# A hybrid decoder layer on one core: in the last block, the last head's scan begun behind its keys, and two heads' output gates projected last

## The chip, the cores and the metric

The kernel runs on one core of one Trainium2 chip. The metric is the device time of one execution in microseconds (us). The core has five engines that run side by side, each in the order of its own instruction queue: TensorE (PE in the profile; its weight loads are PEld) multiplies matrices into PSUM, VectorE (DVE) and ScalarE (ACT) do elementwise work, GpSimd (POOL) does elementwise work in SBUF, and SyncE (SP) issues most of the transfers. ACT issues some transfers as well. An engine waits for another through semaphores; an instruction that waits holds everything behind it in its queue.

## The reference, cut to what matters

One decoder layer over 2048 tokens and 16 meta tokens ahead of them, width 1024, all in float32. The normalized input is projected to everything that two branches and their merge gates need; the branches are a Mamba-2 scan (16 heads) and gated linear attention, GLA (4 heads). Here only GLA matters:

```python
u = rmsnorm(hres, norm_w)
z, xbc, dt_raw, q, k, v, g_gla, a_lr, merge_g = split_cols(u @ w_in, IN_WIDTHS)
log_a = log_sigmoid(a_lr @ gla_gate_w2 + gla_gate_b) / 16
# per head (128 keys, 256 values), in chunks, with state S carried along the sequence:
#   S_t = diag(exp(log_a_t)) S_{t-1} + k_t^T v_t ;  o_t = q_t S_t
y_gla = rmsnorm(o, gla_norm_w) * silu(g_gla)
```

Each head so needs its queries and keys (q, k), its values (v) and its output gate (g_gla, 256 channels). The scan needs q, k and the decays first, v later, and the output gate only in its very last operation. The branch results then go through a second set of products: `sum_b sigmoid(g_b) * (y_b @ w_branch_b)`, `@ w_out`, residual and a last rmsnorm.

## The kernel before

**Two phases.** The first phase computes, in four blocks of 512 tokens, all projections but the merge gates', and both scans; it leaves the branch results (`y_left`) in DRAM. The second phase multiplies large matrices in stages (gate, branch 0, branch 1 for each half of the sequence, then out), with operands that it loads and prepares ahead (`load_a`, `prep_a`, `load_b`, `prep_b`). Each float32 operand is held as a high and a low part, and each product is three matmuls (`accum`, L188 to L190, which all products share in the profile: projections write `pj`, the scans write `pc`, the second phase `psa`, `psb`, `psc`).

**Order in a block.** Eight units follow each other: four groups of the Mamba branch, then four GLA heads, here called heads 0 to 3. Each unit is a generator of projection pieces (`gla_proj`); at each of its `yield`s the loop calls `step()`, which advances every running scan by one step. A scan is put on the list by `begin`. So PE's queue reads: a projection piece, then one step of each scan that runs, then the next piece. PE's and SP's order is the order in which the code is written; the order of ACT, DVE and POOL is set by a scheduler when the program is built, which moves instructions ahead where their operands allow it.

**A GLA head's projection.** Six pieces: queries (24 matmuls of 512 columns), keys (24), values in two halves (48 of 256 columns each), and two gate pieces (24 each). The weights come through four `whl` buffers. A gate piece ends in a tanh on ACT (L661) and a product on DVE (L662) into a `gg` tile, of which there are four. Only then is the head's scan begun.

**A GLA head's scan** (`gla_scan`), step by step: decays applied to keys and queries; six levels (64, 32, 16, 8, 4, 2), each with a subtraction on DVE (L711), two exponentials on ACT (L714, L715), products on DVE (L716, L718), two small matmuls on PE (L726) and a masked copy on DVE (L733); beside these the transposes of the decayed keys (L744) into two `kdt` tiles; pair and diagonal sums (L790), the masked attention, its transposes (L805), two `atp` tiles; then for each of four chunks a *c row*: six accumulations `pc<-tok,kdt` and `pc<-tok,atp`, one product with the state (L816), the state's update on DVE (L817), a copy on ACT (L819) and a sum of squares on ACT (L821). At the end `rstd` on DVE and POOL (L231, L232), a scaling on ACT (L826), eight transposes on PE (L831), the product with the gate on DVE (L832), and the store `y<-gg`, issued by ACT (L835).

PSUM is shared: three banks `pj`, three `pt` (transposes, L790), two `pc`. One scan holds both `kdt` and both `atp`.

**Into the second phase.** Its tiles lie on the first phase's memory. SP issues, behind the last weight, eight `ar` loads, then the `br` loads, of which five fit. POOL makes sums of `ar` (L944 to L947), ACT and DVE split them into high and low parts (L953, L954), and likewise `br` (L929, L930). The first product waits for the first `b`.

When the loop over the blocks has ended, `while running or begun: step()` runs what is left of the scans.

Of the kernel before, what the change touches and what calls it, by code (L numbers as in the profile page):

```python
# [40 lines left out]
def trunk_kernel(ctx: ExitStack, tc: tile.TileContext, xm, xmt, w_feat, w_tok, w_zm, w_br, w_o,  # L41
# [587 lines left out]
            nc.scalar.dma_start(y_left[0][o.b][2 * g + j], yo)  # L629


    def gla_proj(o, h):
        m0 = o.m0
# [8 lines left out]
        yield  # L642
        vh = mk(wk, [P, NCH, 256], F32R, "tok4", bufs=NT4)
        vl = mk(wk, [P, NCH, 256], F32R, "tok4", bufs=NT4)
        vm = None
        pss, places = halves_of(pj, "pj")
        if m0:
            vm = mk(wk, [P, 256], F32, "c1", bufs=NC1)[:META]
            pv5 = bank(pt, "pt")
            places.append((2, pv5[:, :256]))  # L650
        yield from proj_tok(f"v{h}", w_tok[SG + h], o.u, o.starts + [0] * o.ci0, places)
        if m0:
            nc.scalar.activation(vm, pv5[:META, :256], AF.Copy)
        for r, ps in enumerate(pss):
            split(*[t[:, 2 * r:2 * r + 2].rearrange("p c f -> p (c f)") for t in (vh, vl)], ps)
        yield
        gs = []
        for j in range(2):
            ps, = proj_feat(f"g{t0 + 2 + j}", w_feat[t0 + 2 + j], o.segs_real, o.mov)
            gg = mk(wk, [P, BLK], F32, "gg", bufs=4)  # L660
            nc.scalar.activation(gg, ps, AF.Tanh, scale=0.5)  # L661
# [3 lines left out]
        begin(gla_scan(o, h, qs, kf, (vh, vl), vm, gs))  # L665

    def gla_scan(o, h, qs, kf, vt, vm, gs):
        m0, tt = o.m0, o.tt
        gf = o.g_all[:, h, :tt]
        gr = gf[:, m0:]  # L670
# [79 lines left out]
        yield  # L750
        if m0:
            ps = bank(pc, "pc")
            nc.tensor.matmul(ps[:, :256], btm[:META], vm, start=True, stop=True)
            nc.vector.tensor_copy(s_gla[:, h], ps[:, :256])
        level_out(32)
        level_in(8)
# [53 lines left out]
        ssq = mk(sm, [P, 4], F32, "ssq")  # L810
        for c in range(NCH):
            po = bank(pc, "pc")
            vc = [t[:, c] for t in vt]
            accum(po[:, 256:], [t[:, c] for t in kdt], vc, True, True)
            accum(po[:, :256], [t[:, c] for t in atp], vc, True, False)
            nc.tensor.matmul(po[:, :256], qg[:, c * P:(c + 1) * P], s_gla[:, h], start=False, stop=True)  # L816
            nc.vector.scalar_tensor_tensor(s_gla[:, h], s_gla[:, h], egl[:, c:c + 1], po[:, 256:],  # L817
                                           op0=ALU.mult, op1=ALU.add)
            nc.scalar.activation(ot[:, c], po[:, :256], AF.Copy)  # L819
            jk = mk(wk, [P, 256], BF16, "junk", bufs=1)  # L820
            nc.scalar.activation(jk, po[:, :256], AF.Square, accum_out=ssq[:, c:c + 1])  # L821
            if c % 2:
                yield
        r = rstd_of(ssq, 4, 1.0 / 256)
        for c in range(NCH):
            nc.scalar.activation(ot[:, c], ot[:, c], AF.Identity, scale=r[:, c:c + 1])  # L826
        yield
        for j in range(2):
            ps = bank(pt, "pt")
            for c in range(NCH):  # L830
# [365 lines left out]
```

## Time and profile before

| | us |
|---|---|
| median of three timed runs | 2343.2 (2340.65 to 2347.39) |
| the profiled execution | 2339.3 |
| its span, first to last instruction | 2337.5 |
| PE busy | 2247.0 |
| DVE busy | 1572.1 |
| ACT busy | 1187.5 |
| POOL busy | 686.3 |
| mean granted clock of TensorE | 0.985 |

The span is what lies between the first and the last instruction; 1.8 us of the execution lie around it. Busy time is added up per engine, and engines overlap. A row of the timeline reads: start, duration, engine, line, operation, output and inputs, shape, count, and in brackets how long the engine had been idle before and what released it. A row of a group reads: line, engine, operation, tiles, shapes, count, then busy us and mean ns of one, then the idle time ahead of them and what ended it.

### The profile page before, as it was taken

How to read it: one execution, taken by the hardware profiler on the slowest of the kernel's cores; microseconds unless marked ns; L12 is line 12 of the kernel's file. 1: busy time of each engine (PE TensorE's matmuls, PEld its weight loads, DVE VectorE, ACT ScalarE, POOL GpSimd, SP SyncE). 2: the span in 40 equal slices, each digit the busy share in tenths (PEclk: the TensorE clock that was granted, in tenths of full speed). 3: DMA queues.
4: the chain of work that ended last, by engine and by line, in shares of the span. 5: the costliest groups of instructions: out<-in, count | busy, mean ns of one | idle time of the engine just before them, and what ended most of it. 6: DMA issues, size and time to landing. Idle time of an engine off the chain costs nothing.

```text
span 2337.5 us, 36518 instructions
## 1 busy us (share of the span) xinstructions
PE 2247.0 (96%) x12651; PEld 1961.9 (84%) x12651; DVE 1572.1 (67%) x2884; ACT 1187.5 (51%) x2764; POOL 686.3 (29%) x677
## 2 busy tenths in 40 slices
PE   6899999999999999999999999889999999999998
PEld 6889989888888989888988898768888788788786
DVE  5676766676675666576568555664588854788886
ACT  5666654465544455543465443454555454544443
POOL 3344433122221122222122200207433355332441
PEclk9999999999999999999999999989999999999999
DMA  7665865767785666786666645457668776778763
GB/s 256 222 204 199 295 232 200 227 197 235 249 284 185 210 214 216 247 271 210 201 222 217 207 162 168 140 165 235 215 226 281 270 232 204 257 250 279 237 199 108
DMA packets 300937, 515.89 MB, mean 221 GB/s; under 512 B 27616, under 2 KB 143584, under 8 KB 300752
## 3 DMA queue, kind: packets, MB, share of 16 engines
q1 hardware_dynamic: 200080, 401.17, 53.0%
q10 hardware_dynamic: 100672, 112.39, 13.9%
q8 instruction: 99, 1.62, 0.3%
q14 instruction: 86, 0.70, 0.1%
HBM read 366.26 MB, written 147.19 MB: 220 GB/s over the span
## 4 chain that ended last, share of the span: by engine, by line
PE 35%; DMA 7%; DVE 6%; issue 2%; ACT 2%; SPq 0%; POOL 0%; ACTq 0%; DVEq 0%; POOLq 0%
PE psa L188 4%; PE psa L189 4%; PE psa L190 4%; PE pj L188 4%; PE pj L190 4%; PE pj L189 4%; DMA br<-br_t 2%; PE psb L188 2%; PE psb L189 2%; PE psb L190 2%; DVE b L930 1%; DVE a L954 1%; PE psc L189 1%; PE psc L188 1%; PE psc L190 1%
## 5 line engine op out<-in xcount | busy, mean ns | idle before, releaser
L188 PE MATMUL pj<-u,whl 128*128 128x512 f32 (+1 forms) x1184 | 450.7, 381 | 16.1 <-ACT acc L502 8.9
L190 PE MATMUL pj<-u,whl 128*128 128x512 f32 (+1 forms) x1184 | 433.5, 366 | 0.6 <-POOL whl L176 0.6
L189 PE MATMUL pj<-u,whl 128*128 128x512 f32 (+1 forms) x1184 | 433.6, 366 | 0.0
L188 PE MATMUL pj<-whl,u 128*128 128x256 f32 (+1 forms) x992 | 289.0, 291 | 2.7 <-ACT u L251 2.2
L189 PE MATMUL pj<-whl,u 128*128 128x256 f32 (+1 forms) x992 | 282.3, 285 | 0.7 <-POOL whl L176 0.7
L190 PE MATMUL pj<-whl,u 128*128 128x256 f32 (+1 forms) x992 | 282.4, 285 | 0.2 <-DVE u L256 0.2
L188 PEld LDWEIGHTS pj<-u,whl 128*128 128x128 f32 x1184 | 227.5, 192 | 55.5 <-ACT acc L502 10.0
L188 PE MATMUL psa<-b,a 128*128 128x512 f32 x640 | 252.5, 395 | 15.4 <-ACT sn L970 13.5
L190 PEld LDWEIGHTS pj<-u,whl 128*128 128x128 f32 x1184 | 227.2, 192 | 36.8 <-POOL whl L176 0.8
L189 PEld LDWEIGHTS pj<-u,whl 128*128 128x128 f32 x1184 | 227.7, 192 | 33.5
L189 PE MATMUL psa<-b,a 128*128 128x512 f32 x640 | 251.3, 393 | 0.0
L190 PE MATMUL psa<-b,a 128*128 128x512 f32 x640 | 250.9, 392 | 0.0
L954 DVE TENSOR_TENSOR a<-ar,a 128x512 fp32r<-128x512 f32 x160 | 154.5, 972 | 76.6 <-ACT a L953 76.1
L80 POOL TENSOR_TENSOR wr<-wr 128x256 f32<-128x256 f32 x80 | 69.0, 862 | 434.6 <-DMA wr<-u 178.1
L188 PEld LDWEIGHTS pj<-whl,u 128*128 128x128 f32 x992 | 189.8, 191 | 4.0 <-ACT u L251 2.3
L176 POOL TENSOR_TENSOR whl<-wr,whl 128x512 fp32r<-128x512 f32 (+1 forms) x100 | 134.7, 1354 | 195.4 <-ACT whl L175 151.7
L189 PEld LDWEIGHTS pj<-whl,u 128*128 128x128 f32 x992 | 189.9, 191 | 1.3 <-POOL whl L176 0.9
L190 PEld LDWEIGHTS pj<-whl,u 128*128 128x128 f32 x992 | 189.7, 191 | 0.8 <-DVE u L256 0.8
L944 POOL TENSOR_TENSOR as<-ar,ar 128x512 f32<-128x512 f32 x40 | 59.8, 1494 | 416.5 <-DMA ar<-in_w_feat 123.7
L930 DVE TENSOR_TENSOR b<-br,b 128x512 fp32r<-128x512 f32 x196 | 149.3, 785 | 46.1 <-ACT b L929 45.5
L506 DVE SCALAR_TENSOR_TENSOR acc<-cin,hcw,acc 128x512 f32<-128x512 f32 (+1 forms) x192 | 155.4, 809 | 32.6 <-ACT acc L502 31.4
L929 ACT ACTIVATE b<-br 128x512 fp32r<-128x512 f32 x196 | 118.8, 626 | 92.9 <-DMA br<-br_t 35.3
(278 smaller groups left out, 5074.7 us busy)
## 6 DMA issues: line engine op xcount, KB each, us to landing
whl<-k_s SPq DMA_DIRECT2D x96, 512.0 KB, 4.3
whl<-k_g SPq DMA_DIRECT2D x96, 512.0 KB, 4.1
whl<-k_v SPq DMA_DIRECT2D x48, 512.0 KB, 4.3
whl<-k_z SPq DMA_DIRECT2D x36, 512.0 KB, 3.8
wr<-in_w_feat SPq DMA_DIRECT2D x64, 256.0 KB, 4.3
k_s<-whl SPq DMA_DIRECT2D x32, 512.0 KB, 3.7
cb<-cumd ACTq DMA_DIRECT2D x64, 256.0 KB, 5.7
y<-gg ACTq DMA_DIRECT2D x64, 256.0 KB, 4.3
```

The lines of the kernel that those rows point to most:

```text
L80: nc.gpsimd.tensor_tensor(o, x, y, op=ALU.subtract)
L176: nc.gpsimd.tensor_tensor(hl[:, 1], raw, hl[:, 0].bitcast(F32), op=ALU.subtract)
L188: nc.tensor.matmul(ps, sh, mh, start=first, stop=False, **kw)
L189: nc.tensor.matmul(ps, sh, ml, start=False, stop=False, **kw)
L190: nc.tensor.matmul(ps, sl, mh, start=False, stop=last, **kw)
L506: nc.vector.scalar_tensor_tensor(acc, cin[:, k:k + tt], hcw[:, ti, k:k + 1], acc, op0=ALU.mult, op1=ALU.add)
L929: nc.scalar.activation(t[:, 0], raw, AF.Copy)
L930: nc.vector.tensor_tensor(t[:, 1], raw, t[:, 0].bitcast(F32), op=ALU.subtract)
L944: nc.gpsimd.tensor_tensor(s1, a21, a22, op=ALU.add)
L954: nc.vector.tensor_tensor(t[:, 1], src, t[:, 0].bitcast(F32), op=ALU.subtract)
```

## The change

Only the last block's last two heads are touched, and only the order of their work. The projection of a head is cut into three generators (`gla_keys`, `gla_values`, `gla_gates`). Heads 0 and 1, and all heads of the other blocks, run as before. In the last block, head 2's scan is begun behind its values, with its gates not yet projected; head 3's scan is begun behind its keys; then follow head 3's values, head 2's two gate pieces and head 3's two gate pieces. The scan takes values and gates from a dictionary (`got`) that is filled by then.

```diff
+    def gla_proj(o, h):
+        got = {"gs": []}
+        keys = yield from gla_keys(o, h)
+        last = o.b == nblk - 1
+        if last and h == GH - 1:
+            begin(gla_scan(o, h, *keys, got))
+            yield
+            got["v"] = yield from gla_values(o, h)
+            yield
+            yield from gla_gates(o, h - 1, held_gates.pop())
+            yield from gla_gates(o, h, got["gs"])
+        else:
+            yield
+            got["v"] = yield from gla_values(o, h)
+            if last and h == GH - 2:
+                begin(gla_scan(o, h, *keys, got))
+                held_gates.append(got["gs"])
+                yield
+            else:
+                yield
+                yield from gla_gates(o, h, got["gs"])
+                begin(gla_scan(o, h, *keys, got))
...
-    def gla_scan(o, h, qs, kf, vt, vm, gs):
+    def gla_scan(o, h, qs, kf, got):
...
-            vc = [t[:, c] for t in vt]
+            vc = [t[:, c] for t in got["v"][0]]
...
+        gs = got["gs"]
         for j in range(2):
             ps = bank(pt, "pt")
```

In the changed kernel the lines of the scan stand 28 lower (29 from L826 on): L726 is L754, L790 is L818, L816 is L844, L819 is L847, L831 is L860, L953 is L982, L929 is L958. The text uses the numbers from before.

PE, from the last projection matmul of the first phase to the first product of the second, before; of each accumulation of three only the first row stands here:

```order
L190 MATMUL pj_16914<-u_11312,whl_16929 128x512
L805 MATMUL pt_16946<-cst,sq_16907 128x128 x2
L188 MATMUL pc_16953<-tok_2776_16232,kdt_16649 128x256
...
L744 MATMUL pt_17023<-cst,act_16977 128x128 x4
L726 MATMUL pc_17040<-sq_16992 128x128 x2
...
L831 MATMUL pt_17083<-cst,ot_16951 128x128 x4
...
L790 MATMUL pt_17138<-sq_17126,ones_r 128x512
L805 MATMUL pt_17149<-cst,sq_17142 128x128 x2
L188 MATMUL pc_17156<-tok_2851_16673,kdt_17028 128x256
...
L831 MATMUL pt_17217<-cst,ot_17154 128x128 x4
L188 MATMUL psa_17498<-b_2975_17403,a_17415 128x512
```

The same place now:

```order
L190 MATMUL pj_17101<-u_11312,whl_17116 128x512
L188 MATMUL pc_17142<-tok_2846_16605,kdt_16726 128x256
...
L844 MATMUL pc_17154<-s_gla,act_16593 128x256
L860 MATMUL pt_17166<-cst,ot_16994 128x128 x4
L860 MATMUL pt_17172<-cst,ot_16994 128x128 x4
L188 MATMUL pc_17178<-tok_2846_16605,kdt_16726 128x256
...
L844 MATMUL pc_17190<-s_gla,act_16593 128x256
L860 MATMUL pt_17211<-cst,ot_17140 128x128 x4
L860 MATMUL pt_17217<-cst,ot_17140 128x128 x4
L188 MATMUL psa_17498<-b_2975_17403,a_17415 128x512
```

Before, head 2's c rows and all of head 3's scan stood behind the last projection; now head 3's four c rows do, with the transposes of heads 2 and 3.

PE among the projections now, between the second half of head 3's values (`pj<-whl,u`) and head 2's first gate piece (`pj<-u,whl`); `pc_16818` is a c row of head 1, `pc_16830`, `pt_16834` and `pt_16837` belong to head 2, `pc_16848` to head 3:

```order
L844 MATMUL pc_16818<-s_gla,act_16136 128x256
L754 MATMUL pc_16830<-sq_16692 128x128 x2
L818 MATMUL pt_16834<-c_2864_16713,ones_r 128x256
...
L818 MATMUL pt_16837<-sq_16717,ones_r 128x512
...
L754 MATMUL pc_16848<-sq_16731 128x128 x2
...
L188 MATMUL pj_16872<-u_11312,whl_16873 128x512
```

Three scans now have a step between two projection pieces, where two had before.

ACT, from the third c row of head 3 to the first `b` of the second phase, now:

```order
L847 ACTIVATE ot_17140<-pc_17178 128x256
L849 ACTIVATE junk_17188,ssq_17141<-pc_17178 128x256
L982 ACTIVATE a_17426<-ar_17380 128x512
L982 ACTIVATE a_17441<-ar_17367 128x512
L982 ACTIVATE a_17452<-ar_17382 128x512
L982 ACTIVATE a_17467<-as_17374 128x512
L847 ACTIVATE ot_17140<-pc_17190 128x256
L849 ACTIVATE junk_17200,ssq_17141<-pc_17190 128x256
L854 ACTIVATE ot_17140<-ot_17140,rstd_17204 128x256 x4
L982 ACTIVATE a_17525<-as_17389 128x512
L982 ACTIVATE a_17543<-ar_17369 128x512
...
L958 ACTIVATE b_2975_17403<-br_17395 128x512
```

Before, these six preparations (L953 there) stood between head 2's c rows and head 3's levels, and no row stood between head 3's L819, L821 and L826.

More of the change, by code (lines that the diff above doesn't have):

```diff
@@ L641, in gla_proj, with gla_values @@
             nc.scalar.activation(kf[:, a:a + n], ps[:, :n], AF.Copy)
-        yield
+        return qs, kf
+    def gla_values(o, h):
+        m0 = o.m0
         vh = mk(wk, [P, NCH, 256], F32R, "tok4", bufs=NT4)
@@ L752, in gla_scan @@
             ps = bank(pc, "pc")
-            nc.tensor.matmul(ps[:, :256], btm[:META], vm, start=True, stop=True)
+            nc.tensor.matmul(ps[:, :256], btm[:META], got["v"][1], start=True, stop=True)
             nc.vector.tensor_copy(s_gla[:, h], ps[:, :256])
```

10 lines of the change are left out of this document (5 added, 5 removed).

## The prediction

> **What bounds the kernel now.** I read the page first, for the shares and the slices of the span.
>
> ```profile
> span 2337.5 us, 36518 instructions
> PE 2247.0 (96%) x12651; PEld 1961.9 (84%) x12651; DVE 1572.1 (67%) x2884; ACT 1187.5 (51%) x2764; POOL 686.3 (29%) x677
> PEclk9999999999999999999999999989999999999999
> ```
>
> TensorE (PE) is busy nearly everywhere, so what it must do sets the time; VectorE (DVE) and the others can matter only where PE waits for them. One slice has a lower clock. It is the seam between the first phase (projections and scans) and the second (the products of the gate stage), so I asked for busy time by stretch around it. The columns are stretch, length, then busy us of PE, its weight loads, DVE, ACT and POOL (instructions in brackets), granted clock, DMA share and GB/s.
>
> ```profile
> 1300.00:1400.00 100.00, 100.00 (x605) 89.18 (x604) 58.66 (x135) 48.19 (x124) 11.65 (x18) 1.00 0.57 187
> 1443.50:1500.50 57.00, 57.00 (x340) 50.59 (x340) 33.40 (x73) 20.64 (x56) 5.59 (x4) 1.00 0.59 190
> 1500.50:1526.50 26.00, 15.60 (x70) 12.41 (x69) 25.92 (x52) 14.45 (x40) 9.60 (x7) 0.74 0.14 51
> 1526.50:1544.80 18.30, 10.77 (x50) 8.42 (x48) 7.17 (x16) 6.20 (x20) 1.01 (x1) 0.75 0.10 35
> 1544.80:1580.00 35.20, 33.06 (x134) 26.24 (x135) 25.70 (x41) 25.09 (x46) 3.03 (x3) 0.94 0.86 270
> ```
>
> While there are projections PE has no gap (57.00 of 57.00 us) and DVE idles 23.6 us. In the 44.3 us behind them (the tail) PE is busy 26.4 us at a granted clock of 0.74 to 0.75; DVE is full in the first part of it and nearly empty in the second. PE's timeline shows what stands at the edges.
>
> ```profile
> 1500.32 0.39 PE L190 MATMUL pj<-u,whl 128*128 128x512 f32 x1
> 1500.55 0.38 PE L805 MATMUL pt<-cst,sq 128*128 128x128 f32 x2
> 1530.02 0.56 PE L188 MATMUL pc<-tok,kdt 128*128 128x256 f32 x1
> 1536.80 0.68 PE L816 MATMUL pc<-s_gla,act 128*128 128x256 f32 x2
> 1540.66 2.16 PE L831 MATMUL pt<-cst,ot 128*128 128x128 f32 x8 [3.19 <-ACT ot L826]
> 1544.78 0.80 PE L188 MATMUL psa<-b,a 128*128 128x512 f32 x1 [1.96 <-ACT b L929]
> ```
>
> The last projection matmul is followed at 1500.55 by scan work alone: the second half of head 2's scan and all of head 3's. The second phase's first product starts at 1544.78. The tail is a chain through DVE, ACT, POOL and PE, with nothing for PE to do beside it.
>
> **The change, part by part.** No arithmetic is removed or added. The same eight half-weights of head 2's and head 3's gates are loaded and the same matmuls run; they stand elsewhere. Head 2's scan starts behind its values, head 3's behind its keys, so six projection pieces (head 3's values in two halves, four gate pieces) now run beside head 3's scan. In the changed PE order only four c rows of head 3 (the accumulations at L188 to L190 and L816), eight transposes of head 2 and eight of head 3 (L831) stand behind the last projection.
>
> *First term, what PE takes in earlier.* These leave the tail: head 2's L805 and c rows, head 3's L744, its six levels (24 instructions of L726 in the trace), its L790 and L805. Their cost at full clock beside projections comes from starts in the same trace.
>
> ```profile
> 1443.57 1.04 PE L831 MATMUL pt<-cst,ot 128*128 128x128 f32 x8
> 1444.44 1.06 PE L726 MATMUL pc<-sq 128*128 128x128 f32 x8
> 1445.26 0.48 PE L188 MATMUL pj<-u,whl 128*128 128x512 f32 x1
> 1450.81 0.60 PE L726 MATMUL pc<-sq 128*128 128x128 f32 x4
> 1451.96 0.40 PE L188 MATMUL pj<-u,whl 128*128 128x512 f32 x1
> 1457.44 0.38 PE L805 MATMUL pt<-cst,sq 128*128 128x128 f32 x2
> 1457.58 0.48 PE L188 MATMUL pj<-u,whl 128*128 128x512 f32 x1
> 1463.13 0.28 PE L188 MATMUL pc<-tok,kdt 128*128 128x256 f32 x1
> 1465.35 0.58 PE L188 MATMUL pj<-u,whl 128*128 128x512 f32 x1
> 1470.99 0.28 PE L188 MATMUL pc<-tok,kdt 128*128 128x256 f32 x1
> 1473.39 0.60 PE L744 MATMUL pt<-cst,act 128*128 128x128 f32 x4
> 1473.83 0.61 PE L726 MATMUL pc<-sq 128*128 128x128 f32 x4
> ```
>
> Eight L726 take 0.82 us (1444.44 to 1445.26), so 24 take 2.46. L790 is 1450.81 to 1451.96 less four L726: 0.74. L805 is 0.14, twice 0.28. The c rows of one head are 2.22 (1463.13 to 1465.35) and 2.40 (1470.99 to 1473.39), together 4.62. L744 is 0.44. Sum 8.54. Without a stall the last projection would end at 1500.55 + 8.54 = 1509.1.
>
> *Second term, stalls of PE among the projections.* The two scans now run two steps apart instead of six, and share what holds one of them: two `kdt`, two `atp`, two `pc` banks, three `pt` banks. PE obeys its order, so whatever waits for a bank holds the projection behind it. In the changed order a level's L726 stands right behind a pair of c rows at three places, and its bank comes free only when ACT has read the c row before it (L819, L821). The gap can be read at the end of the tail and in the groups of waits.
>
> ```profile
> 1538.03 0.38 ACT L819 ACTIVATE ot<-pc 128x256 f32<-128x256 f32 x1 [0.52 <-DVE s_gla L817]
> 1538.31 0.38 ACT L821 ACTIVATE junk<-pc 128x256 bf16<-128x256 f32 x1
> L726 PEld LDWEIGHTS pc<-sq 128*128 128x128 f32 x24 | 3.8, 237 | 1.9 <-ACT junk L821 1.1 <-DVE c L733 0.8
> ```
>
> L816 starts at 1536.80 and lasts 0.68, L821 ends at 1538.69: 1.2 us, three times, is 3.6 us, and I take 4. Below it lies 0: PE's own work behind a c row covers the lag. Above it lies 10.4, PE's idle time in 1500.50:1526.50 (26.00 less 15.60), where c rows of one head and levels of the next last ran against each other with no projection between. I stay near the lower bound since projections now stand between. DVE's load speaks for that too: 33.40 + 25.92 + 7.17 = 66.5 us of DVE have to fit into some 80, and part of these is inflated by POOL.
>
> ```profile
> L711 DVE TENSOR_TENSOR sq<-g_all 128x512 f32<-128x512 f32 x5 | 5.6, 1117 | 0.0
> L711 DVE TENSOR_TENSOR sq<-g_all 128x512 f32<-128x512 f32 x8 | 6.6, 823 | 0.0
> L718 DVE TENSOR_TENSOR sq<-sq,act 128x128 f32<-128x128 f32 x12 | 6.1, 553 | 0.0
> L718 DVE TENSOR_TENSOR sq<-sq,act 128x128 f32<-128x128 f32 x12 | 2.9, 288 | 0.0
> 1498.73 1.36 POOL L945 TENSOR_TENSOR as<-as,ar 128x512 f32<-128x512 f32 x1
> ```
>
> The first row of each pair is the tail, the second the stretch ahead of it. Beside POOL's sums for the gate stage (the last row is one of eight; POOL is busy 9.60 us in 1500.50:1526.50) L718 took 553 ns against 288. These sums wait for `ar` loads that SP issues behind the last weight, and in POOL's new order they stand behind head 2's `rstd`. So the levels, which are through by then, lose this neighbour, and DVE's L954 in the new tail gets it.
>
> *Third term, the new tail.* From the last projection's end: four c rows and eight L831 at full clock, 4.62 + 0.87 (head 0's eight, 1443.57 to 1444.44) = 5.5 us. Then what follows the last c row now: its L816 ends at 1537.48, the first product starts at 1544.78, 7.3 us. Here ACT's order adds preparations of the second phase: four L953 ahead of the last L819, two between the last L826 and the store, and two L954 on DVE between the last L832s.
>
> ```profile
> 1512.08 1.15 ACT L953 ACTIVATE a<-ar 128x512 fp32r<-128x512 f32 x2
> 1514.07 1.29 DVE L954 TENSOR_TENSOR a<-ar,a 128x512 fp32r<-128x512 f32 x2
> 1542.23 1.41 DVE L832 SCALAR_TENSOR_TENSOR gg<-pt,hgw,gg 128x512 f32<-128x512 f32 x2 [3.25 <-PE pt L831]
> ```
>
> Two L953 take 1.15, so one every 0.52 to 0.58: four take 2.2, of which some 0.8 pass while the last c row runs, leaving 1.3 to 1.4. Two L954 take 1.29 between the L832s, nearly all on the chain. With 2.6 the new tail is 5.5 + 7.3 + 2.6 = 15.4 us. In the old order those seven L953 and L954 ran in the gaps of the tail; that cover is gone. Bounds: 12.8 if they hide again, 19 if the c rows run at the low clock (1530.02 to 1537.48 is 7.46, 2.8 us above 4.62) and POOL slows two L954 as it slowed L718.
>
> [...]
>
> [...]
>
> *SP and stores.* The chain of waits and ACT's timeline show a head's store and who waited for it.
>
> ```profile
> 1488.10 6.31 DMA y<-gg
> 1494.50 0.60 ACT L661 ACTIVATE gg<-pj 128x512 f32<-128x512 f32 x1 [7.02 <-DMA y<-gg]
> ```
>
> Weight loads of the moved gates are issued in the new order with four `whl` buffers as before; each has at least one projection piece (5.5 us) of lead. Head 1's store of `gg` must land before head 3's first gate can be written (L661); it waited 7.02 us in the old order without holding PE, and about 9 us of PE work (c rows 2.22, L726 and L790 1.15, a gate piece 5.5) lie between now. The first `br` loads wait for the last projection in both orders and have the tail to land in. I cost these at nothing; without the cover, one store's landing (6.31 us) would show.
>
> **The sum.** Last projection ends at 1509.1 + 4 = 1513.1; first product at 1513.1 + 15.4 = 1528.5 instead of 1544.78: 16.3 us less. What follows is the same work in the same order. Against the profiled execution (2339.3 us, span 2337.5) that gives 2323.0; the three timed runs lie at 2343.2 in the median, so 2327. With the bounds (stalls 0 to 10.4, tail 12.8 to 19) the gain is between 22.9 and 6.3; without the corners, 22 to 8: the forecast's own range is 2321 to 2335.
>
> **Rivals.**
> - *Clean overlap.* No stall, and the L953 hide: 1509.1 + 12.8 = 1521.9, 22.9 less, 2320.3. For it: DVE idles 23.6 us beside projections. Against it: two banks for two scans. Chance 0.09.
> - *Shared buffers eat most of it.* PE loses 10.4 to 14 us to banks and to DVE's levels, 2333 to 2337. For it: DVE at 25.92 of 26.00 where two scans met. Against it: 57 us of projections between them. Chance 0.15, about half of it beyond what can be told from no change.
> - *It does nothing.* DVE runs ahead already (levels of head 3 are part of the eight L711 in 1443.50:1500.50, ahead of the last projection's end); if DVE's chain sets the tail, the moved PE order only shifts waits: 2340 to 2345. Against it: DVE's 23.6 idle us. Chance 0.07.
> - *Slower: PE stands behind every level.* If each of the twelve levels of heads 2 and 3 must be waited out in order (subtract, two exponentials, three products: about 2.8 us, an estimate from L711, L718 and their neighbours), 12 × 2.8 = 34 us stand among the projections; the first product starts at 1509.1 + 34 + 15.4 = 1558.5, 14 us later, 2357. It decides from 1.7 us per level, where the stalls reach 20 us. For it: a `pt` bank is held from head 3's L744 until head 2 gives up `kdt`. Against it: DVE is asked a step (5 us or more) ahead. Chance 0.05.
>
> **How the numbers follow.** The forecast has 0.64. A measurement of this kernel tells 0.3% (7 us) from no change. Faster: 0.62 of the forecast, 0.09, 0.08 of the second rival and a little of the third, 0.80. Same: the rest of these, 0.14. Slower 0.06. For 8 in 10 the range takes in the clean overlap with some spread of runs (2340.65 to 2347.39 before) and most of the second rival: 2317 to 2339.
>
> **What would show it.** Right: the granted clock near 1.00 until about 1510; a stretch from the last `pj` matmul to the first `psa` of 14 to 17 us instead of 44.3; PE's idle among the projections 2 to 6 us, named by L726 waiting for L821 or L733. Wrong: gaps over 1.7 us ahead of each L726; a tail above 25 us; L661 waiting for the store with a `pj` matmul behind it; or a second phase that takes longer from its first product to the end.

## The result, and the profile after

The changed kernel took 2331.5 us in the median of 22 runs (2319.7 to 2345.2), the kernel before 2341.9 us in 22 runs beside it: a ratio of 0.9952, 95% interval 0.9939 to 0.9964. By the ratio that is some 11 us less; the medians differ by 10.4. A second measurement (10 runs against 18) gave 0.9958 (0.9943 to 0.9974). The forecast was 2327, some 16 us less; its range, 2317 to 2339, holds the result. The profiled execution took 2335.1 us.

The page of the profile after, shares of the span and TensorE's granted clock by slices:

```profile
span 2333.2 us, 36527 instructions
PE 2243.2 (96%) x12651; PEld 1957.1 (84%) x12651; DVE 1562.5 (67%) x2884; ACT 1188.5 (51%) x2764; POOL 680.4 (29%) x677
PEclk9999999999999999999999999999999999999999
```

PE's busy time is the same within 4 us. No slice shows a lower clock any more, though 10 us at half clock are left in the tail (the last section shows them). Around the seam, by stretch (columns as before: length, busy us of PE, weight loads, DVE, ACT and POOL, clock, DMA share, GB/s):

```profile
1443.23:1512.91 69.68, 67.89 (x408) 58.87 (x407) 47.59 (x119) 30.08 (x85) 4.44 (x4) 1.00 0.48 155
1512.91:1530.88 17.97, 8.66 (x49) 6.54 (x47) 10.83 (x18) 9.42 (x26) 8.54 (x8) 0.84 0.30 107
```

The first row starts at head 0's transposes, which stood at 1443.57 before, and ends behind the last projection; the second is the new tail. PE has 1.8 us of gaps in the first row and 9.3 in the second; before, it had none in 57 us and 17.9 in a tail of 44.3. PE's timeline of the changed kernel has the edges (lines are those of the changed kernel: L754 is L726 of before, L844 is L816, L849 is L821, L854 is L826, L860 is L831, L982 is L953):

```profile
1386.79 1.04 PE L626 MATMUL pt<-cst,tok 128*128 128x128 f32 x8
...
1468.81 0.71 PE L754 MATMUL pc<-sq 128*128 128x128 f32 x4 [0.56 <-ACT junk L849]
...
1512.68 0.39 PE L190 MATMUL pj<-u,whl 128*128 128x512 f32 x1
1512.91 0.28 PE L188 MATMUL pc<-tok,kdt 128*128 128x256 f32 x1
...
1517.37 0.38 PE L188 MATMUL pc<-tok,kdt 128*128 128x256 f32 x1 [0.92 <-ACT junk L849]
1519.34 0.70 PE L844 MATMUL pc<-s_gla,act 128*128 128x256 f32 x2
1524.88 2.53 PE L860 MATMUL pt<-cst,ot 128*128 128x128 f32 x8 [4.84 <-ACT ot L854]
1530.88 0.79 PE L188 MATMUL psa<-b,a 128*128 128x512 f32 x1 [3.47 <-ACT b L958]
```

The last projection ends at 1512.9 (forecast 1513.1) and the first product starts at 1530.88 (forecast 1528.5, before 1544.78). The first row is the landmark for all that follows: the last Mamba group's eight transposes, which stand ahead of anything that the change moves (1387.13 in the profile of before). Times counted from it are compared between kernels; of what lies ahead of it single executions differ by up to 15 us.

| us from the landmark to | last projection matmul | first product | third product (first `psc`) | first product of the branch stage | from the first product to the end |
|---|---|---|---|---|---|
| before | 113.2 | 157.7 | 165.4 | 317.6 | 792.7 |
| before, second profile | 113.2 | 158.8 | 167.2 | 320.1 | 800.6 |
| the change | 125.9 | 144.1 | 151.9 | 307.6 | 802.3 |
| the change, second profile | 125.9 | 144.1 | 152.0 | 306.8 | 799.2 |

So the first product comes 13.6 us sooner (14.7 against the second profile), the branch stage 10 to 13 us sooner, and the time falls by 11.

The gate stage lies between those two places. It took 163.5 and 162.7 us with the change, and 160.0 and 161.3 before: 1.3 to 3.5 us of the gain are lost there again. PE's waits name ACT, which reads the product banks (`sn`, L970): 6.3 and 6.5 us in the two profiles of the change, 4.1 and 3.7 us before, from 140 to 320 us behind the landmark. No run tested what makes these waits longer.

### The profile page after: what moved, and what is told of

The parts are those of the page before. It is cut to its first block, busy times and chain, and to the rows that moved or that the text cites. A ratio compares the mean times of both kernels' runs of the same rounds, so it can differ in the third digit from the quotient of the medians.

```text
span 2333.2 us, 36527 instructions
## 1 busy us (share of the span) xinstructions
PE 2243.2 (96%) x12651; PEld 1957.1 (84%) x12651; DVE 1562.5 (67%) x2884; ACT 1188.5 (51%) x2764; POOL 680.4 (29%) x677
## 4 chain that ended last, share of the span: by engine, by line
PE 60%; DMA 13%; DVE 10%; issue 7%; ACT 6%; POOL 3%; SPq 1%; ACTq 0%; POOLq 0%; DVEq 0%
PE pj L188 10%; PE pj L190 10%; PE pj L189 10%; PE psa L188 4%; PE psa L189 4%; PE psa L190 4%; DMA br<-br_t 2%; PE psb L190 2%; PE psb L189 2%; PE psb L188 2%; PE pc L754 1%; PE pc L591 1%; DMA acc<-in_xmt 1%; DMA br<-gate_t 1%; DVE b L959 1%
## 5 line engine op out<-in xcount | busy, mean ns | idle before, releaser
L983 DVE TENSOR_TENSOR a<-ar,a 128x512 fp32r<-128x512 f32 x160 | 155.2, 977 | 81.4 <-ACT a L982 80.9
L958 ACT ACTIVATE b<-br 128x512 fp32r<-128x512 f32 x196 | 118.5, 625 | 98.3 <-DMA br<-br_t 36.1
```

The lines of the kernel that those rows point to most:

```text
L958: nc.scalar.activation(t[:, 0], raw, AF.Copy)
L983: nc.vector.tensor_tensor(t[:, 1], src, t[:, 0].bitcast(F32), op=ALU.subtract)
```

## The experiments

The time of a whole run scatters by 10 us and more, so the parts are read at the four places of the table; the ratio of the timed runs stands beside them where there is one. The expectations count the runs in the order in which they were made, which is not the order of this text; what is called the third run, the seventh and the ninth is named by its edit too.

**Two halves.** First, head 2 alone: its scan behind its values, its gates last; head 3's scan behind its own gates as before.

```diff
-        if last and h == GH - 1:
+        yield
+        got["v"] = yield from gla_values(o, h)
+        if last and h == GH - 2:
             begin(gla_scan(o, h, *keys, got))
+            held_gates.append(got["gs"])
             yield
...
         else:
             yield
...
+            yield from gla_gates(o, h, got["gs"])
+            begin(gla_scan(o, h, *keys, got))
+            if last and h == GH - 1:
+                yield from gla_gates(o, h - 1, held_gates.pop())
```

> Only head 2 is changed: its scan begins behind its values and its gates are projected behind head 3's gates; head 3's scan begins behind its own gates as before. Measured from the last Mamba group's eight transposes (L626) to the first product of the second phase (the seam): 157.65 us before, 144.09 with the whole change. Theory (what stays behind the last projection costs the length of its chain, what goes beside projections costs PE's matmul time and a small stall): head 2's c rows go among the projections (4.8 us and about 1 of stall), head 3's whole scan stays in the tail (28.4 us in the profile of before, from its L744 to the first product, and about 1 for its first level): seam 148.6, between 146 and 151, some 9 us of gain. Rival (DVE's load sets the tail, so only taking head 3's levels out shortens it): seam at or above 154.

Last projection 120.4, first product 154.7, branch stage 315.5, ratio 0.9973 (0.9955 to 0.9991). The first product gains 3.0 us, not 9: the rival's number. DVE's timeline of this run shows what stood there, its tail starting at 1501:

```profile
1502.32 1.22 DVE L738 TENSOR_TENSOR sq<-sq,act 128x256 f32<-128x256 f32 x1
1503.46 1.55 DVE L740 TENSOR_TENSOR sq<-sq,act 128x128 f32<-128x128 f32 x2
...
1511.06 0.41 DVE L738 TENSOR_TENSOR sq<-sq,act 128x256 f32<-128x256 f32 x1
...
1512.20 0.48 DVE L740 TENSOR_TENSOR sq<-sq,act 128x128 f32<-128x128 f32 x2
```

DVE was busy 18.67 of the 20 us from 1501 on, most of it with head 3's scan. GpSimd's sums for the second phase ran from 1498.1 to 1508.7, and the first two rows, beside them, took three times what the last two took without. My 28.4 us for head 3's scan was counted from PE's first operation of it; in the profile of before DVE had begun these levels ahead of that, beside head 2's c rows.

Second, head 3 alone. Its scan begins behind the first half of its values. Directly behind its keys was not tried: it would run one step behind head 2's scan, and its transposes would stand in PE's queue ahead of the c rows of head 2 that free the `kdt` tiles. Head 3's early start as in the change needs head 2's.

```diff
+        yield
         if last and h == GH - 1:
+            values = gla_values(o, h)
+            next(values)
             begin(gla_scan(o, h, *keys, got))
             yield
+            got["v"] = yield from values
+        else:
             got["v"] = yield from gla_values(o, h)
...
+        yield
+        yield from gla_gates(o, h, got["gs"])
+        if not (last and h == GH - 1):
+            begin(gla_scan(o, h, *keys, got))
```

> Only head 3 is changed: its scan begins behind the first half of its values (behind its keys it would run one step behind head 2's scan, whose buffers it shares), head 2 is as before. Theory (length of the chain): two of head 3's three steps of levels go among the projections, head 2's c rows and head 3's stay in the tail one after the other; last projection about 2 us later, tail about 29 us: seam 145 to 148, some 10 to 12 us of gain. So the two halves do not add up: 9 and 11 alone, 13.6 together. Rival (each half has its own share of the 13.6 us): with the first run at 9, this one gains 4 to 5 and the seam is 153.

Last projection 117.5, first product 153.1, branch stage 316.5, ratio 0.9994 (0.9971 to 1.0017). The first product gains 4.6 us, again not my 10 to 12; the number is the rival's, but its premise, a gain of 9 us from head 2 alone, had failed. The two halves give 3.0 and 4.6 and the whole 13.6, so neither theory holds: the whole is more than its halves, and 6 us come only when both are there. DVE's timeline of this run shows the same neighbour:

```profile
1503.87 1.76 DVE L734 TENSOR_TENSOR sq<-g_all 128x512 f32<-128x512 f32 x1
1505.56 2.62 DVE L741 TENSOR_TENSOR sq<-sq,act 128x128 f32<-128x128 f32 x2
```

With either half alone some levels stay in the tail, beside GpSimd's sums. With both they are through before the sums begin, as DVE's last masked copy of a level and GpSimd's first sum show in the changed kernel:

```profile
1498.77 0.45 DVE L761 COPY_PREDICATED c<-msk,pc 128x256 f32<-128x256 uint8 x1 [0.31 <-PE pc L754]
```

```profile
1510.38 1.29 POOL L973 TENSOR_TENSOR as<-ar,ar 128x512 f32<-128x512 f32 x1
```

Beside the sums DVE's operations were longer than the same ones without by some 3.4 us in the first run and 6 us in the second (estimates, added up from their rows). So the sums can be a good part of what each half lacks; that they are all of it is not shown.

**The neighbour by itself.** The kernel before, with nothing moved but GpSimd's two sets of sums, which wait for head 3's `rstd`:

```diff
         r = rstd_of(ssq, 4, 1.0 / 256)
+        if o.b == nblk - 1 and h == GH - 1:
+            nc.gpsimd.tensor_tensor(behind, r, mhalf[:, :4], op=ALU.pow)
...
+            if self.name == "gate0" and n < 2:
+                nc.gpsimd.tensor_tensor(s1[:, 0, :4], behind, mhalf[:, :4], op=ALU.pow)
             nc.gpsimd.tensor_tensor(s1, a21, a22, op=ALU.add)
```

> The kernel before, with GpSimd's sums for the second phase (L944 to L947, two sets) held back behind head 3's rstd by two tiny operations on GpSimd; nothing else is moved. In the profile of before these sums run from 1497 to 1509 beside DVE's levels, and DVE's L711, L716, L718 and L237 took 11.4 us there that take 4.0 elsewhere. Theory (these 7.4 us are a part of the tail, and the change gained some of its 13.6 us by moving the sums off the levels): the stretch from the last projection to the first product falls from 44.5 to 37 to 39 us, seam (last L626 to first product) 150 to 152, about a half of the change's gain without the change. Rival (DVE's levels are hidden behind head 2's c rows there): seam 155 to 158.

First product 149.0, tail 35.6 us instead of 44.2: 8.7 us sooner without moving anything on PE, more than the 6 to 8 us that the theory gave. Groups on DVE, of before where the sums run beside the levels (1497:1509.1):

```profile
L711 DVE TENSOR_TENSOR sq<-g_all 128x512 f32<-128x512 f32 x3 | 4.2, 1404 | 0.0
L718 DVE TENSOR_TENSOR sq<-sq,act 128x128 f32<-128x128 f32 x4 | 4.2, 1086 | 0.0
```

and of this run at the same work (1498:1509.5; its lines are one higher), then where the sums run now (1537:1549, the preparation of the gate stage's `b`):

```profile
L712 DVE TENSOR_TENSOR sq<-g_all 128x512 f32<-128x512 f32 x5 | 3.4, 686 | 0.0
L719 DVE TENSOR_TENSOR sq<-sq,act 128x128 f32<-128x128 f32 x8 | 2.0, 287 | 0.0
...
L933 DVE TENSOR_TENSOR b<-br,b 128x512 fp32r<-128x512 f32 x8 | 10.3, 1361 | 0.0
```

And yet no change of the time shows: ratio 1.0003 (0.9984 to 1.0023). The third product gained 6.3 us of the 8.7, and the branch stage, at 316.0, 1.6 us (4.1 against the second profile of before). The sums had found another victim: L933 took 1361 ns beside them, and 688 ns per operation as the same group in the profile of before. That stands ahead of the third product; what takes back the rest in the gate stage was not traced. So part of the 13.6 us of the change is this: it takes the levels away from under the sums, and the sums then fall into a stretch where DVE is not full (10.83 of 17.97 us). How the 13.6 us divide between the two causes these runs do not say; the changed kernel with the sums held back was not run.

**The new tail** (the third run). The preparations of the second phase, which stood between head 3's last operations, asked for behind them: ACT and DVE are held to the order in which the code is written, in the end of the scans and in the first preparations. A third edit, not shown, writes the first preparation of `a` ahead of the first of `b`. As built, all but one stand behind head 3's stores.

```diff
+    with tc.manual_schedule(engines={mybir.EngineType.PE, mybir.EngineType.SP, mybir.EngineType.Activation,
+                                     mybir.EngineType.DVE}):
         while running or begun:
             step()
...
-        run(-1)
+        with tc.manual_schedule(engines={mybir.EngineType.Activation, mybir.EngineType.DVE}):
+            run(-1)
```

> The changed kernel, but ACT and DVE take the end of the scans and the preparations behind it in the order of the code: all L953/L954 but the first stand behind head 3's stores instead of between its last operations. Theory (the four L953 ahead of the last c row's copy cost 2.1 us and the two L954 between the last two gate products 1.8 us on the chain): the stretch from the last projection to the first product falls from 18.0 to about 14.1 us, seam 140.2 (139.5 to 141.5), and the gate stage's first products run up to 2 us slower for operands prepared later. Rival (they only fill time in which the chain waits for something else): seam 143 to 144.

Last projection 125.9 as with the change, first product 141.3, third 149.0, branch stage 302.6, ratio 0.9928 (0.9900 to 0.9956, from four runs). The first product is inside the theory's range. The tail falls by 2.8 of the 3.9 us expected, and the gate stage is not slower for it. ACT's and DVE's timelines of the changed kernel show what was removed, and one cost that I had not seen:

```profile
1513.60 0.62 ACT L982 ACTIVATE a<-ar 128x512 fp32r<-128x512 f32 x1
1516.53 0.38 ACT L847 ACTIVATE ot<-pc 128x256 f32<-128x256 f32 x1 [2.31 <-PE pt L860]
...
1519.96 1.67 ACT L982 ACTIVATE a<-ar 128x512 fp32r<-128x512 f32 x3
1521.52 0.62 ACT L982 ACTIVATE a<-as 128x512 fp32r<-128x512 f32 x1
1522.04 0.38 ACT L847 ACTIVATE ot<-pc 128x256 f32<-128x256 f32 x1
```

```profile
1520.08 0.48 DVE L845 SCALAR_TENSOR_TENSOR s_gla<-s_gla,egl,pc 128x256 f32<-128x256 f32 x1 [0.79 <-PE pc L844]
...
1526.60 0.75 DVE L861 SCALAR_TENSOR_TENSOR gg<-pt,hgw,gg 128x512 f32<-128x512 f32 x1 [3.40 <-PE pt L860]
1527.26 1.27 DVE L983 TENSOR_TENSOR a<-as,a 128x512 fp32r<-128x512 f32 x1
1528.46 0.68 DVE L983 TENSOR_TENSOR a<-ar,a 128x512 fp32r<-128x512 f32 x1
1529.06 0.74 DVE L861 SCALAR_TENSOR_TENSOR gg<-pt,hgw,gg 128x512 f32<-128x512 f32 x1
```

Four L982 keep the last c row's copy (L847) until 1522.04, though the state update that it waits for otherwise (L845, first row of the second fence) was done at 1520.56: 1.5 us. Two L983, one of them slowed by a GpSimd sum (1.27 against 0.68), keep the second gate product until 1529.06, though its transposes were done at 1527.41 (1524.88 + 2.53): 1.6 us. The sum, 3.1, is near the 2.8 us that this run gained. The unseen cost is the second row: the copy of head 3's first c row waits 2.31 us for head 2's transposes. There is one `ot` tile, and head 2 still holds it. The third c row then waits 0.92 us for its bank.

**The banks.** The sum of squares (the seventh run) reads the copy in SBUF instead of the PSUM bank:

```diff
-            nc.scalar.activation(jk, po[:, :256], AF.Square, accum_out=ssq[:, c:c + 1])
+            nc.scalar.activation(jk, ot[:, c] if o.b == nblk - 1 else po[:, :256], AF.Square,
+                                 accum_out=ssq[:, c:c + 1])
```

> The changed kernel, but in the last block the sum of squares (L821) reads the copy in SBUF instead of the PSUM bank, so the bank comes free about 0.3 us after each c row's copy instead of 0.7. Theory (the levels' wait for the two pc banks is the stall among the projections): from the last L626 to the last projection matmul 125.89 us becomes 124.4 to 125.0. Rival (the banks wait for DVE's masked copies and the order of c rows, not for L821): 125.6 to 126.2.

Last projection 125.2, 0.7 us sooner: between the two expectations, nearer the theory. The waits of PE from the landmark to the last projection, of the changed kernel and then of this run:

```profile
PE pc L754 <- ACT junk L849: 1.3, 3, 0.6
```

```profile
PE pc L754 <- ACT ot L847: 0.5, 1, 0.5
```

L849 was the holder that the prediction named, and reading the copy instead is worth 0.7 us. First product 143.2, but third product 151.9, as with the change; branch stage 305.2. Then three `pc` banks and two `pt` banks, in the whole first phase:

```diff
-    pt = first.enter_context(tc.tile_pool(name="pt", bufs=3, space=bass.MemoryType.PSUM))
-    pc = first.enter_context(tc.tile_pool(name="pc", bufs=2, space=bass.MemoryType.PSUM))
+    pt = first.enter_context(tc.tile_pool(name="pt", bufs=2, space=bass.MemoryType.PSUM))
+    pc = first.enter_context(tc.tile_pool(name="pc", bufs=3, space=bass.MemoryType.PSUM))
```

> The changed kernel with three pc banks and two pt banks instead of two and three, for the whole first phase. Theory (the scans' two pc banks are the stall among the projections, about 4 us): from the last L626 to the last projection 125.89 us becomes 122.5 to 124.3, and no L726 waits for L821 there any more. Rival (DVE's masked copies and the order in which a c row's three parts come are the wait, or two pt banks stall as much): 125 or more.

Last projection 131.9, 6.0 us later; first product 149.8; one run of 2347.4 us. PE's waits there:

```profile
PE pt L818 <- DVE c L820: 2.6, 2, 1.7
PE pt L818 <- DVE kdt L237: 0.9, 1, 0.9
```

No L754 waits any more, as the theory said, and the pair sums wait for `pt` banks instead, as the rival said. Whether a bank more, with none taken away, would remove the whole stall stays open.

**TensorE's clock in the tail.** 36 small matmuls behind the last c row and 26 behind head 3's transposes, whose result nobody reads:

```diff
+            ps = bank(pj, "pj")
+            for _ in range(n):
+                nc.tensor.matmul(ps[:, :P], ones_r, ones_r, start=True, stop=True)
```

> The changed kernel with 36 small matmuls (ones by ones, 128 columns, into a projection bank that nobody reads) behind the last c row and 26 behind head 3's transposes, so that TensorE does not stand still in the tail. Theory (the low granted clock in the tail costs time): clock near 1.00 there; head 3's eight transposes take about 1.0 us instead of 2.53 and the first products follow each other at 0.69 us instead of 1.28; seam 144.09 becomes 142.5 to 143.3, and the third product (first psc) comes at 148.0 to 149.5 from the last L626 instead of 151.93. Rival (the products wait for b's preparation, and the transposes for ACT, whatever the clock): first psc at 151 to 152.5.

First product 145.9, 1.8 us later; third 152.5; branch stage 306.8. The numbers are the rival's, but not for its reason: the clock fell all the same, and the transposes still took 2.53 us. Windows of 1 us in this run:

```profile
1526.00:1527.00 1.00, 1.00 (x12) 1.00 (x10) 0.45 (x2) 0.04 (x1) 0.47 (x1) 1.00 0.00 0
1527.00:1528.00 1.00, 0.26 (x3) 0.12 (x2) 0.00 (x0) 0.42 (x2) 1.00 (x2) 1.00 0.00 0
...
1529.00:1530.00 1.00, 1.00 (x5) 0.78 (x5) 0.15 (x1) 1.00 (x3) 1.00 (x2) 0.50 0.00 0
...
1535.00:1536.00 1.00, 1.00 (x7) 1.00 (x6) 1.00 (x3) 1.00 (x3) 0.00 (x0) 0.50 0.25 14
...
1538.00:1539.00 1.00, 1.00 (x5) 0.77 (x5) 0.22 (x1) 0.89 (x2) 0.00 (x0) 0.87 0.92 248
```

The clock fell to a half at 1528, with PE idle there for 0.9 us, and stayed there until 1538, with PE busy by its records from 1528.14 on, at first with transposes and small matmuls. The 26 matmuls took 5.79 us and held the first product up. Since the clock was not kept up, this run does not tell what the low clock costs in the tail.

**The change carried on** (the fourth run). Head 1's scan behind its values, head 2's and head 3's behind their keys, so that eight pieces run beside head 3's scan and only its eight transposes stand behind the last projection:

```diff
         if last and h == GH - 1:
+            return
+        keys = yield from gla_keys(o, h)
+        if last and h == GH - 2:
             begin(gla_scan(o, h, *keys, got))
+            yield
+            got3 = {"gs": []}
+            keys3 = yield from gla_keys(o, h + 1)
+            begin(gla_scan(o, h + 1, *keys3, got3))
             yield
             got["v"] = yield from gla_values(o, h)
             yield
-            yield from gla_gates(o, h - 1, held_gates.pop())
+            got3["v"] = yield from gla_values(o, h + 1)
+            yield
             yield from gla_gates(o, h, got["gs"])
+            yield from gla_gates(o, h + 1, got3["gs"])
         else:
...
-            if last and h == GH - 2:
+            if last and h == GH - 3:
                 begin(gla_scan(o, h, *keys, got))
...
```

> The change carried on: in the last block head 1's scan begins behind its values, head 2's behind its keys, head 3's behind its keys with head 2's values still to come, so eight projection pieces run beside head 3's scan instead of six and only its eight transposes stand behind the last projection. Theory: two more pairs of c rows among the projections (4.6 us) and up to 2 us more of stalls, so the last projection ends about 5.6 us later than with the change; tail 5 to 7 us instead of 18.0; seam 137.7 (136 to 140), time about 6 us below the changed kernel. Rival (three scans two steps apart share two kdt, two atp and two pc banks and PE waits for them): more than 8 us of idle PE among the projections, seam above 142.

Last projection 136.4, first product 142.6, tail 6.2 us; but the third product only at 155.1, later than with the change, and the branch stage at 311.2. Ratio 0.9937 (0.9913 to 0.9961), not to be told from that of the change. The last projection moved by 10.5 us where 5.6 were expected. The first product misses the theory's 136 to 140 and is the rival's (above 142), but PE's gaps from the landmark to the last projection came to 5.0 us, not to the rival's 8. PE's timeline shows what followed the first product, and DVE's what stood there:

```profile
1534.40 0.79 PE L188 MATMUL psa<-b,a 128*128 128x512 f32 x1 [4.97 <-ACT b L964]
1538.90 0.79 PE L189 MATMUL psa<-b,a 128*128 128x512 f32 x1 [3.70 <-DVE b L965]
...
1539.92 0.63 PE L188 MATMUL psa<-b,a 128*128 128x512 f32 x1
```

```profile
1531.16 6.48 DVE L989 TENSOR_TENSOR a<-ar,a 128x512 fp32r<-128x512 f32 x4
```

Four preparations of `a`, each 1.6 us beside GpSimd's sums, stood on DVE ahead of DVE's part of the first `b`, for which PE's second matmul waited 3.70 us (L965). The same order once more, with the preparations behind the end (as in the third run, the new tail) and the squares from SBUF (as in the seventh):

> The fourth run's order (eight pieces beside head 3's scan), with the sums of squares read from SBUF and with ACT and DVE in the order of the code behind the loop, so that the first preparations are one a and then the b. There the first product started at 142.58 from the last L626 but the second of its four parts came 5.5 us later, since four L954 (6.48 us beside GpSimd's sums) stood ahead of the second b. Theory (the preparations' order is what ate the gain): last projection 1 to 2 us earlier (135), third product (first psc) at 146 to 149 instead of 155.08. Rival (the b loads land only 6 us after the last projection and set it): first psc at 150 to 152.

Last projection 134.2, first product 138.4, third 149.1, branch stage 305.5: just outside the theory's 146 to 149, and short of the rival's 150. ACT's timeline shows what ends the wait for the second `b` now:

```profile
1522.18 0.63 ACT L967 ACTIVATE b<-br 128x512 fp32r<-128x512 f32 x1 [0.90 <-DVE gg L868]
1525.02 1.26 ACT L967 ACTIVATE b<-br 128x512 fp32r<-128x512 f32 x2 [2.20 <-DMA br<-u]
```

It is the load that the rival named, with sums still beside DVE: the second `b` could be split only at 1525.02, 6.4 us behind the start of the last projection matmul (1518.63). So in this order a still shorter tail would wait for the `b` loads; an order with these loads issued sooner was not tried.

**Three edits on the change** (the ninth run). The third run's order, the squares from SBUF, and head 3's scan output in two tiles of its own:

```diff
+        if o.b == nblk - 1 and h == GH - 1:
+            oq = [mk(wk, [P, 2, 256], F32, "sq", bufs=NSQ) for _ in range(2)]
+            ot = [oq[c // 2][:, c % 2] for c in range(NCH)]
```

> The changed kernel with three edits together: the preparations behind the end of the scans (third run), the sums of squares read from SBUF (seventh run), and head 3's scan output in two tiles of its own instead of the one ot tile that it shares with head 2. Theory (the three costs are separate): first product (from the last L626) at 141.3 less 0.7 less 0.5 to 1.0, so 139.4 to 140.3 against 144.09 with the change alone, and 0.9925 of the time before (0.990 to 0.9945), some 6 us below the changed kernel. Rival (ot's single buffer costs nothing beside the other two, or the end of the chain takes back what its middle gains): 140.6 to 141.5.

First product 140.3, third 147.6, branch stage 303.9, 2327.7 us in the median, ratio 0.9941 (0.9919 to 0.9963), against 0.9958 (0.9943 to 0.9974) for the changed kernel beside it. The first product lies between the two expectations: the last projection, at 125.2, shows the squares' 0.7 us again, and what is left for the tiles is 0.3 of the 0.5 to 1.0. The wait for `ot` is gone, and one for DVE's order stands in its place:

```profile
1512.35 0.79 DVE L991 TENSOR_TENSOR a<-ar,a 128x512 fp32r<-128x512 f32 x1
1513.06 0.47 DVE L850 SCALAR_TENSOR_TENSOR s_gla<-s_gla,egl,pc 128x256 f32<-128x256 f32 x1
```

The one preparation that was still hoisted, and head 2's two gate products, stand ahead of the second c row's state update. This version beats the kernel before; that it beats the changed kernel shows at the places (3.8 us at the first product, 3 at the branch stage) and not in the times, whose intervals overlap. At the branch stage the third run did as well (302.6).

**Both kernels once more**, for the 9.6 us by which the first pair of profiles differs behind the first product.

> The changed kernel once more, for a second profile. If the seam is a property of the order: last projection at 125.7 to 126.1 from the last L626, first product at 143.8 to 144.4. From the first product to the end it had 802.3 us where before had 792.7: if that comes from the change (operands that come later, or other collisions), it is 799 to 806 again; if it is the spread of single executions, anywhere from 792 to 806.

> The kernel before once more, for a second profile. Seam 157.4 to 157.9 if it is a property of the order. From the first product to the end: 790 to 795 again if the 9.6 us between the two profiles come from the change, 795 to 806 if they are the spread of single executions.

The places of the change repeat within 0.1 us up to the third product; before's first product came 1.1 us later in its second profile, outside what was expected of it. From the first product to the end before took 800.6 us and the change 799.2: the 9.6 us did not repeat and are the spread of single executions. Over all fourteen profiles this part lies between 792.7 and 805.2 us, in no order that the edits would explain.

## Why the prediction was right, and where not

*First and second term.* Moved PE work 8.5 us and stalls 4: together 12.5, measured 12.7 (125.9 less 113.2). The 8.54 was not measured by itself, so the stalls come out at 4.2 as a difference. Only 1.8 us of it are gaps in the records. PE's busy time up to the last projection grew by 10.9 us (113.4 to 124.3), 2.4 more than the 8.54; whether that is moved work priced too low or rows that run on into a wait was not taken apart. The names were right, L726 waiting for L821, but taking L821 off the bank gave 0.7 us, where three times 1.2 had been put down to the bank. That the stalls came so near to 4 is in good part luck. The fear of a gap ahead of every level was not borne out: the longest was 0.6 us.

*Third term.* This one was mis-sized: 15.4 us forecast, 18.0 measured, inside its bounds of 12.8 and 19, and it is nearly the whole error at the first product (13.6 us sooner instead of 16.3). By pieces: 5.5 us for c rows and transposes came to 7.1. I had listed the buffers that two scans share (`kdt`, `atp`, `pc`, `pt`) and left out `ot`, whose one tile held the copy 2.31 us and the third c row 0.92. That `ot` is the cause of the 1.6 us is not shown, though: with tiles of its own, in the ninth run, this stretch still took 7.0 us (1508.54 to 1515.55); there the second state update stood behind other work on DVE. The stretch behind the last c row was 10.8 instead of 7.3 + 2.6 (1520.04, the end of the last L844, to 1530.88): L982 and L983 stand exactly where the order put them and cost 1.5 and 1.6 us, together 3.1 where 2.6 were allowed; without them, in the third run, this stretch took 7.5 us (1513.25 to 1520.77) and the first product gained 2.8. The clock was as assumed, 1.00 in the c rows, a half only from 1525 on.

*The cover of the rest.* No wait for a store held a projection. What follows the first product was forecast as the same work in the same order: its whole length shows no difference beyond the spread, but its gate stage was 1.3 to 3.5 us longer, which the sum had at nothing. The gain at the branch stage, 10 to 13 us, is the gain of the timed runs, 11.

*DVE beside GpSimd's sums.* The prediction saw the sums come to stand beside the two late L954, and let them cost something in the upper bound of the new tail alone. One of the two was stretched, by 0.6 us (1.27 against 0.68). But this neighbour was far more important than I let it be at another place: the levels in the tail of before lost to the same neighbour most of the 8.7 us that the first product gained when the sums were held back, and the prediction mentioned this as inflation without pricing it. My account by what is left behind the last projection took this part in without pricing it: it came near for the whole change, where no level is left beside the sums, and failed by some 6 us on each half, where some are.

*The rivals.* Clean overlap and the bank rival both missed the last projection; "it does nothing, DVE's chain sets the tail" was half right on each half alone (3.0 and 4.6 us) and wrong on the whole.

*Signs and readings.* Of the signs that were to show the forecast right, the clock held; the stretch behind the last projection, 18.0 us, lies outside the 14 to 17 that were given, and PE's gaps among the projections, 1.8 us, just below the 2 to 6. Two readings were loose, and nothing rested on them: "nearly empty" for DVE was 7.17 of 18.30 us, and "those seven" L953 and L954 are eight in the list above it.

## What to carry to other kernels

Cost a tail by the engine that is full in it, not by the matmuls that PE has there: here DVE's levels and GpSimd's sums beside them set it, and half the change gave a quarter to a third of the gain. When a neighbour's work is moved, look for its next victim before booking the gain; held back from the levels, the sums gave 8.7 us at the first product, of which 6.3 were left at the third and 1.6 to 4.1 at the branch stage. And list every tile that two overlapping units share, the last one in the chain too; freeing one may only bring up the next wait, as with `ot`.

## What the runs showed of the hardware that was not expected

Beside GpSimd's sums three groups of DVE operations took two to four times as long as without: 1404 against 686 ns (L711, 128x512) and 1086 against 287 ns (L718, 128x128), in the kernel before and with the sums held back, and 1361 against 688 ns (the preparation of `b`, 128x512 with an fp32r output), with the sums held back and in the kernel before. GpSimd's sums changed less: in the profile of before they took 1.3 to 1.7 us each.

In the run with the small matmuls the granted clock fell within 0.9 us of the end of 36 back-to-back 128-column matmuls and stayed at a half for 10 us of busy records; the window from 1538 on shows 0.87 again. In the changed kernel it also stayed at a half for 10 us, with 3.5 us of them idle; windows of 1 us there:

```profile
1524.00:1525.00 1.00, 0.12 (x1) 0.12 (x1) 0.00 (x0) 0.68 (x2) 1.00 (x2) 1.00 0.00 0
1525.00:1526.00 1.00, 0.93 (x3) 0.38 (x3) 0.00 (x0) 1.00 (x4) 1.00 (x2) 0.55 0.00 0
...
1535.00:1536.00 1.00, 1.00 (x5) 0.77 (x5) 0.55 (x1) 0.98 (x2) 0.00 (x0) 0.83 0.77 279
1536.00:1537.00 1.00, 1.00 (x6) 0.82 (x5) 0.79 (x2) 0.66 (x2) 0.00 (x0) 1.00 0.98 356
```

Measured in steps of half a microsecond around the seam, the stretch at half clock of the changed kernel comes to 10.2 us (1525.1 to 1535.3) in its first profile; the first profile of the kernel before has four, of 10.2, 3.4, 6.8 and 6.8 us, between 1504.7 and 1549.2. So the length of one stretch does not carry over to the next, not even in one execution. Why the clock stayed at a half in the run with the small matmuls, where matmuls filled PE's records, these runs do not show.
